# First tiles of the second matrix, tail weights and a fifth weight buffer in a macaron FFN–mixer encoder layer on one core

## Chip, core and metric

The kernel runs on one NeuronCore of a Trainium2 chip. The metric is the device time of one execution in microseconds (us). Three runs of the kernel before gave 1299.45 to 1301.09 us, with a median of 1300.53 us. A profile was taken of one more execution, which took 1301.27 us.

The core has engines that run side by side: TensorE (PE: matrix products, with weight loads as a row of their own, PEld), VectorE (DVE), ScalarE (ACT), GpSimd (POOL) and SyncE (SP), whose queue issues most of the transfers. Each engine takes its instructions in a fixed order. PE writes its results to eight PSUM banks.

## What is computed

One encoder layer over 512 positions with 16 meta tokens ahead of them (528 columns), 1024 channels, in float32. The second FFN needs only the 512 real columns.

```python
def swiglu(x, wi, wo):
    a, b = jnp.split(x @ wi, 2, axis=-1)
    return (jax.nn.silu(a) * b) @ wo
...
    h = jnp.concatenate([meta, x], axis=1)
    for l in range(DEPTH):
        n = norm_gains[l]
        h = h + 0.5 * rmsnorm(swiglu(rmsnorm(h, n[0]), ffn1_wi[l], ffn1_wo[l]), n[1])
        h = h + rmsnorm(hybrid_mixer(rmsnorm(h, n[2]), ...), n[3])
        h = h + 0.5 * rmsnorm(swiglu(rmsnorm(h, n[4]), ffn2_wi[l], ffn2_wo[l]), n[5])
    return h[:, N_META:]
```

The mixer has an input projection, three branches (a Fourier branch, a short convolution, and a delta rule that runs over chunks of 64 positions in both directions), and an output projection. The hidden width of each FFN is 2816, which is 22 tiles of 128 for `a` and 22 for `b`.

## The kernel before

Data lies with channels on the 128 partitions and positions along the free dimension, so 1024 channels are eight tiles (`KD`). A float32 factor is split into a rounded part and its rest: ACT casts (`wh`, `gh`, `x`'s first part), DVE subtracts (`wl`, `gl`, `x`'s second part). Each product is then three matmuls, written in `mm`. Every matmul of that kind carries line L144.

**Weights.** `load` fetches one weight tile into a staging tile `ws` (two of them), casts it on ACT and takes the rest on DVE (L230 and L231). The results `wh` and `wl` come from the pool `wp`, with four buffers each. `load` asks the scheduler to place this work earlier than written. `double` loads the weights for two output tiles of the second matrix at once.

**Order.** PE's instructions run as they are written. On the other engines a scheduler sets the order by priorities: `high_priority(n)` moves what is inside it n instructions up. `URGENT` is 450, `XAHEAD` 150.

**Stages.** `start` makes the first normalised input, and three units of the first matrix (a unit is one output tile over eight steps). `ffn` copies those raw (`raw`), makes five more units, and forms from them four gated tiles g = silu(a)·b (`silu`, `pair`; the split is at L235 and L236). `seven` scales the input (L555) and forms the sums that a Strassen-like scheme needs: it turns the two halves of the columns and of the channels into seven products. `rest` makes the last four splits of these sums. `both` computes two output tiles of the second matrix over the first four hidden tiles: all steps but the last of the two tiles, then the last step and the eviction of each. After the first `both` comes `rest`, then the second `both`. Then the long loop of Strassen products begins (`one`, `five`, `two`, `six`, `seven`, `four`), with second-matrix tiles between them. In FFN1 a tile has two halves of 264 columns, each in its own PSUM bank. In FFN2 both halves lie in one bank and matmuls are 512 wide, apart from the products and edges, which run 256 wide.

**Tail and edge.** The last hidden chunk goes through `tail`, whose eight output tiles are computed first for the first half of the columns, then for the second. `leave_y` copies a finished tile and adds its square to `acc`. `stat` turns `acc` into the factor of a norm: matmuls with ones, a square root on ACT, a reciprocal on DVE (L290), matmuls that spread the factor over the partitions, and a copy to `r` (L286). `edge` then makes the next stage's input: `step(i, k)` is, for half i and channel tile k, two DVE operations (L405, L407), an ACT copy (L411) and a DVE rest (L412). Three units of the next stage run on these inputs as they come: first half, then second. `early` puts the first half's `stat` between the matmuls of the second half's tail tiles. Edge 1 lies ahead of the mixer, edge 2 ahead of FFN2. `xstat` gathers the sums of squares of the new input (L302 on ACT, L303 on DVE) for the norm's factor `rx`. `finish` is the last norm.

The first term of `early`, the number of steps before the first half's `stat`, and the calls that set what runs first in an FFN are:

```python
            for _ in range(5):
                yield
            next(post[0])
...
        both(0, 0)
        with self.tc.high_priority(XAHEAD):
            rest()
        for m in range(2, FIRST, 2):
            both(0, m)
```

PSUM has two pools of four banks, `pb` (`big`) and `pd` (`dnp`). The mixer uses both, and shares `wp` with the FFNs.

## Time and profile before

| | |
|---|---|
| median of three runs | 1300.53 us (1299.45 to 1301.09) |
| profiled execution | 1301.27 us |
| its span in the trace | 1299.4 us |
| instructions in the trace | 22964 |
| mean granted TensorE clock | 0.996 |
| HBM read, written | 120.68 MB, 7.37 MB |

The profiled execution is 1.87 us longer than its span. Stages by the trace, in us from the span's start: start and first units to about 60; second-matrix first tiles to 74; loop of FFN1 to 357; its tail and edge 1 to 401; mixer to 880; output projection and edge 2 to 951; start of FFN2 to 994; its loop to 1262; finish to the end. A busy share by itself tells little here, since PE is busy nearly all of the time; the short stretches in which PE waits, or in which its clock is halved, are what can be read.

A line of a timeline is: start in us, duration in us, engine, line, operation, output and input, size, count, and in brackets the idle time ahead of it with what released it. A line of the windows view is: the stretch, its length, the busy time and number of instructions of PE, PEld, DVE, ACT and POOL, then the granted clock as a share of full speed, the DMA share and GB/s. A line of the waits view is: who waits for whom, us in total, number of waits, the longest.

### The profile page before, as it was taken

Reading aid. Unit: us, or ns where it says so; the run is one execution under the profiler, and the core shown is the slowest. Engines: PE = TensorE matmul, PEld = TensorE weight load, DVE = VectorE, ACT = ScalarE, POOL = GpSimd, SP = SyncE. Lnnn points to the kernel's source line nnn. Section 1 sums busy time; section 2 is a strip of 40 time slices with the busy share of each in tenths; the row PEclk is TensorE's granted clock in tenths of the full one; section 3 lists DMA queues with packets and bytes.
Section 4 is the critical chain, followed back from the end, with each engine's and each line's share of the span. In section 5 each row is a group of like instructions: output and inputs, shape, how many; then the busy total and the mean of one; then the engine's idle time right before and its main releaser. Section 6 shows DMA issues by size and latency. Waiting matters only on the chain.

```text
span 1299.4 us, 22964 instructions
## 1 busy us (share of the span) xinstructions
PE 1275.8 (98%) x9071; PEld 1157.2 (89%) x9071; DVE 942.5 (73%) x1867; ACT 615.9 (47%) x1208; POOL 13.4 (1%) x28
## 2 busy tenths in 40 slices
PE   9999999999999999999999999999999999999997
PEld 9999999999989988778977777887887999999997
DVE  7968777776568779658788678554789787777654
ACT  7555444434376543343632534334557554444436
POOL 0000000000000000000000000000100000000000
PEclk9999999999999999999999999999999999999999
DMA  7233333332244222312222212235433333333213
GB/s 250 80 106 99 98 98 98 98 101 71 82 163 160 82 82 73 110 63 82 66 66 66 66 58 73 82 97 178 147 117 102 107 106 99 106 98 94 86 49 130
DMA packets 70207, 129.53 MB, mean 100 GB/s; under 512 B 15820, under 2 KB 24140, under 8 KB 70100
## 3 DMA queue, kind: packets, MB, share of 16 engines
q1 hardware_dynamic: 64244, 124.40, 29.9%
q10 hardware_dynamic: 5088, 1.57, 0.5%
q0 software_dynamic: 768, 2.10, 0.4%
q8 instruction: 71, 1.16, 0.4%
q14 instruction: 36, 0.29, 0.1%
HBM read 120.68 MB, written 7.37 MB: 99 GB/s over the span
## 4 chain that ended last, share of the span: by engine, by line
PE 88%; DVE 7%; ACT 3%; issue 1%; DMA 1%; SPq 0%; DVEq 0%; ACTq 0%
PE pb L144 54%; PE pd L144 32%; DVE wl L231 1%; PE pd L148 1%; DVE acc L303 1%; DVE s L405 1%; ACT pb L346 1%; DVE h L407 1%; DVE x L412 0%; DMA ws<-in_wout 0%; ACT wh L230 0%; DVE l L236 0%; ACT sy L335 0%; DVE acc L336 0%; DMA h<-in_xT 0%
## 5 line engine op out<-in xcount | busy, mean ns | idle before, releaser
L144 PE MATMUL pb<-x,wh 128*128 128x264 f32 (+3 forms) x1568 | 357.4, 331 | 8.1 <-DVE x L412 3.6
L144 PEld LDWEIGHTS pb<-x,wh 128*128 128x128 f32 x1568 | 247.8, 190 | 40.9 <-DVE x L412 6.1
L144 PE MATMUL pb<-x,wl 128*128 128x264 f32 (+3 forms) x784 | 220.1, 326 | 0.0
L230 ACT CAST wh<-ws 128x1024 fp32r<-128x1024 f32 (+2 forms) x116 | 109.3, 945 | 176.5 <-PE pb L144 138.5
L144 PE MATMUL pd<-x,wh 128*128 128x264 f32 (+2 forms) x1040 | 192.1, 285 | 0.0
L235 ACT CAST wh<-wf 128x1024 fp32r<-128x1024 f32 x108 | 113.5, 1051 | 153.6 <-PE pd L144 122.3
L144 PE MATMUL pb<-gh,h 128*128 128x264 f32 (+1 forms) x768 | 172.8, 321 | 0.0
L144 PEld LDWEIGHTS pd<-x,wh 128*128 128x128 f32 x1040 | 160.5, 189 | 1.9
L236 DVE TENSOR_TENSOR wl<-wf,wh 128x1024 fp32r<-128x1024 f32 x108 | 132.0, 1223 | 39.4 <-ACT wh L235 39.0
L231 DVE TENSOR_TENSOR wl<-ws,wh 128x1024 fp32r<-128x1024 f32 (+2 forms) x116 | 126.2, 1090 | 33.1 <-ACT wh L230 32.7
L144 PEld LDWEIGHTS pb<-x,wl 128*128 128x128 f32 x784 | 134.1, 190 | 12.8 <-DVE wl L375 0.2
L144 PE MATMUL pd<-x,wl 128*128 128x264 f32 (+2 forms) x520 | 143.9, 284 | 0.0
L144 PEld LDWEIGHTS pb<-gh,h 128*128 128x128 f32 x768 | 120.9, 188 | 10.4
L144 PE MATMUL pb<-gl,h 128*128 128x264 f32 (+1 forms) x384 | 102.6, 321 | 0.0
L144 PEld LDWEIGHTS pd<-x,wl 128*128 128x128 f32 x520 | 96.3, 188 | 0.3
L144 PE MATMUL pd<-h,wh 128*128 128x264 f32 (+1 forms) x294 | 82.1, 282 | 0.0
L144 PE MATMUL pd<-l,wh 128*128 128x264 f32 (+1 forms) x288 | 81.5, 283 | 0.0
L144 PE MATMUL pd<-h,wl 128*128 128x264 f32 (+1 forms) x288 | 81.3, 282 | 0.0
L680 DVE TENSOR_TENSOR y<-y,pb 128x264 f32<-128x264 f32 (+1 forms) x128 | 48.7, 421 | 26.9 <-PE pb L144 26.9
L144 PEld LDWEIGHTS pb<-gl,h 128*128 128x128 f32 x384 | 63.6, 188 | 4.6
L144 PE MATMUL pb<-y,wh 128*128 128x512 f32 x192 | 61.7, 403 | 0.0
L230 ACT CAST h<-ws 128x1024 fp32r<-128x1024 f32 (+1 forms) x34 | 33.9, 1001 | 56.4 <-PE pb L144 50.5
(311 smaller groups left out, 2355.1 us busy)
## 6 DMA issues: line engine op xcount, KB each, us to landing
wf<-in_wi SPq DMA_DIRECT2D x144, 256.0 KB, 2.8
ws<-in_wo SPq DMA_DIRECT2D x64, 256.0 KB, 2.9
ws<-in_win SPq DMA_DIRECT2D x32, 512.0 KB, 3.2
ws<-in_wg SPq DMA_DIRECT2D x24, 512.0 KB, 3.2
ws<-in_wi SPq DMA_DIRECT2D x13, 512.0 KB, 3.3
ws<-in_wo SPq DMA_DIRECT2D x32, 192.0 KB, 2.5
ws<-in_wout SPq DMA_DIRECT2D x8, 512.0 KB, 3.2
h<-in_xT SPq DMA_DIRECT2D x10, 264.0 KB, 3.0
```

Source lines behind the costliest of these rows:

```text
L144: return self.e.matmul(out, lhsT, rhs, **kw)
L148: return self.e.transpose(*a)
L230: nc.scalar.copy(h[:, :n], st[:, :n])
L231: nc.vector.tensor_tensor(l[:, :n], st[:, :n], h[:, :n].bitcast(F32), op=ALU.subtract)
L235: self.nc.scalar.copy(h, src)
L236: self.nc.vector.tensor_tensor(l, src, h.bitcast(F32), op=ALU.subtract)
L303: V.tensor_tensor(acc, acc, sq, op=ALU.add)
L346: self.nc.scalar.copy(p, first[:, m, :w])
L405: V.scalar_tensor_tensor(t, ya[0][i][:, k, :W], self.gains[:, gpost, k:k + 1], r[:, c], op0=ALU.mult, op1=ALU.mult)
L407: V.tensor_tensor(hT[:, k, c], hT[:, k, c], t, op=ALU.add)
L680: V.tensor_tensor(y, y, p, op=ALU.add)
```

## The change

There are nine parts.

1. `wp` has five buffers of each of `wh` and `wl` instead of four.
2. `leave_y` takes the square of a tile before it copies the tile.
3. In `edge` after an FFN, the loads of the next stage's weights are written ahead of the tail tiles.
4. The first half's `stat` comes after seven steps of the second half's tail instead of five, in edge 1 and in `finish`.
5. `edge` serves as many units as it is given weights. Edge 2 is given four, so the unit of `wi[KF + 1]` leaves `ffn` and runs in the edge (48 matmuls of 256 columns instead of 24 of 512).
6. `xstat` in edge 2 has a priority of 60 instead of 450.
7. In `ffn`, scaling, silu and gating of the first three hidden tiles are urgent.
8. The four first tiles of the second matrix run together: all steps but the last of the four tiles, then the last step and eviction of each. The first two use `pd` banks. `rest` comes before them.
9. The tail's weights are split into the room of `h3` and `l3` (input sums of the Strassen scheme), no longer into `wp`.

```diff
-        self.wp = e(tc.tile_pool(name="wp", bufs=4))
+        self.wp = e(tc.tile_pool(name="wp", bufs=5))
...
-            if gain is None:
-                ACT.copy(y[i][:, m, :w], p)
-            else:
-                ACT.activation(y[i][:, m, :w], p, AF.Copy, scale=self.gains[:, gain, m:m + 1])
             if m == 0:
                 ACT.activation(acc[i], p, AF.Square)
             else:
...
+            if gain is None:
+                ACT.copy(y[i][:, m, :w], p)
+            else:
+                ACT.activation(y[i][:, m, :w], p, AF.Copy, scale=self.gains[:, gain, m:m + 1])
...
         tiles, tx, tc, more = tail()
+        if more:
+            ws = [self.load(a) for a in nxt]
         for t in tiles:
...
-            for _ in range(5):
+            for _ in range(7 if more else 5):
                 yield
...
-        ws = [self.load(a) for a in nxt]
-        os = [self.outs(C), self.outs(C), self.outs(C, self.dnp)]
+        if not more:
+            ws = [self.load(a) for a in nxt]
+        n = len(nxt)
+        os = [self.outs(C, self.dnp if i == 2 else None) for i in range(n)]
...
-            for j in range(3):
-                k = i - (LAG if j == 2 else 0)
+            for j in range(n):
+                k = i - (LAG if j >= 2 else 0)
...
-        self.xstat(C, hT, rx, *((XF, URGENT) if keep is not None else ()))
+        self.xstat(C, hT, rx, *((XF, 60) if keep is not None else ()))
...
-        for t, o in zip((a, b, a1), os):
+        for t, o in zip((a, b, a1, b1), os):
             self.raw(t, o)
-        o, o2, o3 = (self.unit(wi[i], x, C, new=n) for i, n in ((KF + 1, None), (2, None), (KF + 2, self.dnp)))
+        o = None if len(os) == 4 else self.unit(wi[KF + 1], x, C)
+        o2, o3 = self.unit(wi[2], x, C), self.unit(wi[KF + 2], x, C, new=self.dnp)
         self.drain()
-        for t in (a, b):
-            V.tensor_tensor(t[:, u], t[:, u], self.rx[:, u], op=ALU.mult)
-        silu(a)
-        pair(0, a[:, u], b[:, u])
...
+        with urgent():
+            for t in (a, b):
+                V.tensor_tensor(t[:, u], t[:, u], self.rx[:, u], op=ALU.mult)
+            silu(a)
+            pair(0, a[:, u], b[:, u])
...
-        both(0, 0)
-        with self.tc.high_priority(XAHEAD):
-            rest()
-        for m in range(2, FIRST, 2):
-            both(0, m)
+        ws = [double(0, m) for m in range(0, FIRST, 2)]
+        with self.tc.high_priority(XAHEAD):
+            rest()
+        us = [second(0, m, ws[m // 2], self.dnp if m < 2 else None) for m in range(FIRST)]
+        for ks, _, n in us:
             ks(range(n - 1))
-            ks2(range(n - 1))
+        for ks, evict, n in us:
             ks([n - 1])
             evict()
-            ks2([n - 1])
-            evict2()
...
-            ws = [double(fin, m) for m in range(0, KD, 2)]
+            q = KD * P * 3 // 4
+            h, l = (self.t(self.gp, i, [P, 3, 4, HN], F32R).rearrange("p a k c -> p (a k c)") for i in ("h3", "l3"))
+            at = lambda a, i: a[:, i * q:(i + 1) * q].rearrange("p (k c) -> p k c", c=P)
+            ws = [double(fin, m, (at(h, m // 2), at(l, m // 2))) for m in range(0, KD, 2)]
...
-        pre = k.edge(REAL, hT, ya, 3, 4, tail, to_ffn, [wi[0], wi[KF], wi[1]], k.keep)
+        pre = k.edge(REAL, hT, ya, 3, 4, tail, to_ffn, [wi[0], wi[KF], wi[1], wi[KF + 1]], k.keep)
```

Lines of the kernel after are shifted: L528 of before (the scaling of a unit out of its PSUM bank) is L532 after, L555 is L559, L627 (a times b) is L631, L640 and L643 are L646 and L649, L336 (the sum of squares) is L332, and the weight sums L603 to L609 are L607 to L613.

The change moves instructions on DVE at three places. The first is the start of FFN1 on DVE, before. `pb_389` and `pb_390` are the two banks of the unit `wi[KF + 1]`, `ev` are the tiles in which a and b are kept, and `h` is the input that `seven` scales.

```order
L528 TENSOR_TENSOR ev_376<-pb_389,rx_90 128x264
L555 SCALAR_TENSOR_TENSOR h_87<-h_87,gains_77,rx_90 128x528 x6
L231 TENSOR_TENSOR wl_743<-ws_741,wh_742 128x1024
L555 SCALAR_TENSOR_TENSOR h_87<-h_87,gains_77,rx_90 128x528 x2
L236 TENSOR_TENSOR l_78_725<-h_87,h_77_724 128x1056
L640 TENSOR_TENSOR ev_375<-ev_375,rx_90 128x528
L236 TENSOR_TENSOR l_78_725<-h_87,h_77_724 128x1056
L640 TENSOR_TENSOR ev_375<-ev_375,rx_90 128x528
L643 TENSOR_TENSOR ev_376<-ev_376,rx_90 128x528
L528 TENSOR_TENSOR ev_376<-pb_390,rx_90 128x264
```

The same place on DVE after the change:

```order
L532 TENSOR_TENSOR ev_376<-pb_389,rx_90 128x264
L231 TENSOR_TENSOR wl_743<-ws_741,wh_742 128x1024
L646 TENSOR_TENSOR ev_375<-ev_375,rx_90 128x528 x2
L649 TENSOR_TENSOR ev_376<-ev_376,rx_90 128x528
L532 TENSOR_TENSOR ev_376<-pb_390,rx_90 128x264
L559 SCALAR_TENSOR_TENSOR h_87<-h_87,gains_77,rx_90 128x528
```

The eight scalings of the input and two of its splits, which stood between the two banks, now come behind the second bank, one or three at a time among the gating of the first tiles.

The second place is edge 1 on DVE, before: the first steps of the first half, from the reciprocal of its norm on. `wl` with 1024 elements are the splits of the mixer's first three weight tiles, `acc_740` the second half's sum of squares.

```order
L290 RECIPROCAL rt_4382<-rt_4382 88x3
L336 TENSOR_TENSOR acc_740<-acc_740,sy_4389 128x264
L231 TENSOR_TENSOR wl_4544<-ws_4542,wh_4543 128x1024
L336 TENSOR_TENSOR acc_740<-acc_740,sy_4404 128x264
L405 SCALAR_TENSOR_TENSOR s_4414<-y_737,gains_77,r_4206 128x264
L405 SCALAR_TENSOR_TENSOR s_4419<-y_737,gains_77,r_4206 128x264
L336 TENSOR_TENSOR acc_740<-acc_740,sy_4439 128x264
L407 TENSOR_TENSOR h_4197<-h_4197,s_4414 128x264
L407 TENSOR_TENSOR h_4197<-h_4197,s_4419 128x264
L231 TENSOR_TENSOR wl_4550<-ws_4548,wh_4549 128x1024
L336 TENSOR_TENSOR acc_740<-acc_740,sy_4454 128x264
L412 SCALAR_TENSOR_TENSOR x_4208<-h_4197,gains_77,x_4207 128x264
```

And on DVE after:

```order
L290 RECIPROCAL rt_4406<-rt_4406 88x3
L332 TENSOR_TENSOR acc_740<-acc_740,sy_4415 128x264
L405 SCALAR_TENSOR_TENSOR s_4432<-y_737,gains_77,r_4206 128x264
L405 SCALAR_TENSOR_TENSOR s_4437<-y_737,gains_77,r_4206 128x264
L407 TENSOR_TENSOR h_4197<-h_4197,s_4432 128x264
L407 TENSOR_TENSOR h_4197<-h_4197,s_4437 128x264
L332 TENSOR_TENSOR acc_740<-acc_740,sy_4450 128x264
L405 SCALAR_TENSOR_TENSOR s_4442<-y_737,gains_77,r_4206 128x264
L412 SCALAR_TENSOR_TENSOR x_4208<-h_4197,gains_77,x_4207 128x264
```

The three weight splits now stand ahead of the first sum of squares; from the reciprocal to the first half's sixth rest none is left.

The third place is the end of edge 2 on DVE, before: the last three rests of the second half and what stands around them. `sx` are the squares that `xstat` adds, and `wf` the weight tiles of FFN2's first pair, of which L603 and its kind form sums.

```order
L405 SCALAR_TENSOR_TENSOR s_10342<-y_9677,gains_77,r_9873 128x256
L303 TENSOR_TENSOR acc_10380<-acc_10380,sx_10394 128x256
L412 SCALAR_TENSOR_TENSOR x_9875<-h_9674,gains_77,x_9874 128x256
L303 TENSOR_TENSOR acc_10380<-acc_10380,sx_10397 128x256
L412 SCALAR_TENSOR_TENSOR x_9875<-h_9674,gains_77,x_9874 128x256
L407 TENSOR_TENSOR h_9674<-h_9674,s_10342 128x256
L603 TENSOR_TENSOR wf_10728<-wf_10728,wf_10731 128x512
L303 TENSOR_TENSOR acc_10380<-acc_10380,sx_10400 128x256
L412 SCALAR_TENSOR_TENSOR x_9875<-h_9674,gains_77,x_9874 128x256
```

The same place on DVE after the change, up to the last rest but one:

```order
L609 TENSOR_TENSOR wf_10748<-wf_10747,wf_10749 128x512
L303 TENSOR_TENSOR acc_10406<-acc_10406,sx_10426 128x256
L303 TENSOR_TENSOR acc_10429<-acc_10429,sx_10431 128x256
L405 SCALAR_TENSOR_TENSOR s_10370<-y_9671,gains_77,r_9867 128x256
L303 TENSOR_TENSOR acc_10429<-acc_10429,sx_10434 128x256
L611 TENSOR_TENSOR wf_10749<-wf_10750,wf_10749 128x512
L303 TENSOR_TENSOR acc_10429<-acc_10429,sx_10437 128x256
L407 TENSOR_TENSOR h_9668<-h_9668,s_10370 128x256
L303 TENSOR_TENSOR acc_10429<-acc_10429,sx_10440 128x256
L613 TENSOR_TENSOR wf_10750<-wf_10748 128x512
L303 TENSOR_TENSOR acc_10429<-acc_10429,sx_10443 128x256
L412 SCALAR_TENSOR_TENSOR x_9869<-h_9668,gains_77,x_9868 128x256
```

Before, the sums of squares stood one or two at a time between the rests from the first half on. Now all fourteen stand behind the second half's third rest, and the four weight sums among them.

More of the change, by code (lines that the diff above doesn't have):

```diff
@@ L446, in edge @@
             step(1, k)
-            for j in range(3):
+            for j in range(n):
                 self.mm(os[j].half[1:], ws[j], x, k, k, k == 0, k == KD - 1)
-        self.xstat(C, hT, rx, *((XF, URGENT) if keep is not None else ()))
+        self.xstat(C, hT, rx, *((XF, 60) if keep is not None else ()))
         return x, os
@@ L473, in early @@
         def early():
-            for _ in range(5):
+            for _ in range(7):
                 yield
@@ L634, in ffn @@
         a, b, a1, b1 = e0[:, 0], e0[:, 1], e1[:, 0], e1[:, 1]
-        for t, o in zip((a, b, a1), os):
+        for t, o in zip((a, b, a1, b1), os):
             self.raw(t, o)
-        o, o2, o3 = (self.unit(wi[i], x, C, new=n) for i, n in ((KF + 1, None), (2, None), (KF + 2, self.dnp)))
+        o = None if len(os) == 4 else self.unit(wi[KF + 1], x, C)
+        o2, o3 = self.unit(wi[2], x, C), self.unit(wi[KF + 2], x, C, new=self.dnp)
         self.drain()
-        for t in (a, b):
-            V.tensor_tensor(t[:, u], t[:, u], self.rx[:, u], op=ALU.mult)
-        silu(a)
-        pair(0, a[:, u], b[:, u])
-        V.tensor_tensor(a1[:, u], a1[:, u], self.rx[:, u], op=ALU.mult)
-        silu(a1)
-        self.scaled(b1, o)
-        pair(1, a1[:, u], b1[:, u])
-        e = self.ev()
-        self.scaled(e[:, 0], o2)
-        silu(e[:, 0])
-        self.scaled(e[:, 1], o3)
-        pair(2, e[:, 0, u], e[:, 1, u])
+        with urgent():
[3 more added lines that the diff above has]
+            pair(0, a[:, u], b[:, u])
+            V.tensor_tensor(a1[:, u], a1[:, u], self.rx[:, u], op=ALU.mult)
+            silu(a1)
+            if o is None:
+                V.tensor_tensor(b1[:, u], b1[:, u], self.rx[:, u], op=ALU.mult)
+            else:
+                self.scaled(b1, o)
+            pair(1, a1[:, u], b1[:, u])
+            e = self.ev()
+            self.scaled(e[:, 0], o2)
+            silu(e[:, 0])
+            self.scaled(e[:, 1], o3)
+            pair(2, e[:, 0, u], e[:, 1, u])
         e = self.ev()
@@ L663, in ffn, with second @@
         later = []
-        def second(ci, m, w):
+        def second(ci, m, w, new=None):
             n = len(CHUNKS[ci])
-            o = self.outs(C)
+            o = self.outs(C, new)
             def ks(r):
@@ L687, in double @@
             return self.load([wo[i][:, c.start:c.stop] for i in (m, m + 1)], len(c), to)
-        def both(ci, m):
-            w = double(ci, m)
-            (ks, evict, n), (ks2, evict2, _) = second(ci, m, w), second(ci, m + 1, w)
+        ws = [double(0, m) for m in range(0, FIRST, 2)]
[3 more added lines that the diff above has]
+        for ks, _, n in us:
             ks(range(n - 1))
-            ks2(range(n - 1))
+        for ks, evict, n in us:
             ks([n - 1])
             evict()
-            ks2([n - 1])
-            evict2()
-        both(0, 0)
-        with self.tc.high_priority(XAHEAD):
-            rest()
-        for m in range(2, FIRST, 2):
-            both(0, m)
         hx = self.t(self.xp, "h", [P, KD, L], F32R).rearrange("p k c -> p (k c)")
```

## The prediction

> **What bounds the kernel now.** I read the page's engine shares first, then its chain of work that ended last, then PE's waits, and last the windows, cut at the places where PE waits.
>
> ```profile
> PE 1275.8 (98%) x9071; PEld 1157.2 (89%) x9071; DVE 942.5 (73%) x1867; ACT 615.9 (47%) x1208; POOL 13.4 (1%) x28
> ...
> PE 88%; DVE 7%; ACT 3%; issue 1%; DMA 1%; SPq 0%; DVEq 0%; ACTq 0%
> ```
>
> PE is busy for 98% and is 88% of the chain that ended last, so the matmuls themselves set the time. The change takes none of them away. What it can win is in the other 12% of the chain, where PE waits for DVE or ACT.
>
> ```profile
> PE pb L144 <- DVE x L412: 3.6, 9, 0.8
> PE pb L144 <- DVE ev L528: 2.8, 1, 2.8
> PE pb L144 <- DVE gl L236: 1.7, 2, 1.2
> ...
> PE pd L144 <- DVE acc L336: 0.8, 1, 0.8
> PE pb L144 <- ACT x L411: 0.8, 1, 0.8
> PE pd L144 <- DVE rt L290: 0.7, 1, 0.7
> ```
>
> These rows sum to 10.4 us, and each belongs to an FFN's start, an edge or the finish. The windows add what such waits do to the clock:
>
> ```profile
> 40.00:47.00 7.00, 4.69 (x39) 4.47 (x37) 7.00 (x10) 4.17 (x5) 0.00 (x0) 1.00 0.25 75
> 47.00:51.00 4.00, 3.56 (x18) 3.56 (x19) 3.92 (x7) 2.19 (x4) 0.00 (x0) 0.57 0.30 78
> 51.00:74.00 23.00, 21.78 (x177) 21.39 (x175) 21.21 (x27) 14.20 (x21) 0.00 (x0) 1.00 0.15 49
> ...
> 366.00:381.00 15.00, 12.42 (x97) 11.30 (x95) 10.74 (x24) 14.42 (x37) 0.20 (x2) 1.00 0.36 106
> 381.00:388.00 7.00, 6.51 (x42) 6.31 (x43) 5.25 (x14) 2.87 (x8) 0.00 (x0) 0.76 0.51 203
> ...
> 412.00:880.00 468.00, 466.05 (x3094) 386.66 (x3093) 348.20 (x912) 195.38 (x430) 4.26 (x6) 1.00 0.25 78
> ...
> 910.00:953.00 43.00, 40.08 (x305) 37.20 (x304) 34.48 (x82) 25.20 (x62) 8.77 (x16) 1.00 0.39 129
> 953.00:1000.00 47.00, 45.51 (x217) 37.26 (x217) 41.98 (x50) 28.89 (x43) 0.00 (x0) 1.00 0.32 101
> ```
>
> In 40–47 and 51–74 DVE is busy nearly throughout while PE is not: there DVE is the bound. In 468 us of the mixer PE idles 1.95 us. Twice PE's clock drops, to 0.57 over 4 us and to 0.76 over 7 us, which costs 4.0·0.43 = 1.7 us each time (7.0·0.24 = 1.7).
>
> **Term 1, start of FFN1: −4.9 us.** The rows of PE, then of DVE:
>
> ```profile
> 44.41 0.28 PE L144 MATMUL pb<-x,wh 128*128 128x264 f32 x1
> 47.44 1.03 PE L144 MATMUL pb<-x,wh 128*128 128x264 f32 x3 [2.75 <-DVE ev L528]
> ...
> 66.78 0.51 PE L144 MATMUL pb<-gl,wh 128*128 128x264 f32 x2 [1.22 <-DVE gl L236]
> ...
> 74.00 0.65 PE L144 MATMUL pd<-h,wh 128*128 128x264 f32 x4
> ```
> ```profile
> 35.52 0.43 DVE L528 TENSOR_TENSOR ev<-pb,rx 128x264 f32<-128x264 f32 x1
> 36.19 4.17 DVE L555 SCALAR_TENSOR_TENSOR h<-h,gains,rx 128x528 f32<-128x528 f32 x6 [0.24 <-ACT rx L286]
> ...
> 46.96 0.43 DVE L528 TENSOR_TENSOR ev<-pb,rx 128x264 f32<-128x264 f32 x1
> ...
> 67.81 1.22 DVE L236 TENSOR_TENSOR wl<-wf,wh 128x1024 fp32r<-128x1024 f32 x1
> ```
>
> PE waits 2.75 us for a bank that DVE empties at 46.96, because the eight scalings of h and two splits of them stand ahead. Urgent gating moves these behind it: now one weight split and three scalings of `ev` stand there, about 1.2 + 3·0.6 = 3 us from 36, so the bank is free near 39.5 and PE needs it at 44.5. The wait goes, with the half clock behind it (1.6). The wait for `gl` goes too, since 72 matmuls of 0.12 us (the four at 74.00 take 0.65, 0.28 of it the last one's length), four tiles by three steps, now run ahead of the fourth `gl`, where 36 did. PE would then reach the first loop product (74.00) about 6.2 us sooner, at 67.8.
>
> DVE's work has only been re-ordered, though. From 36.2 on, 42 operations up to and with the first product's weight split stand in the new order, 31.3 us by their sizes: 0.34 us for 264 columns from start to start, 0.6 to 0.7 for 528, 1.15 for 1024 and more (the 27 of the window 51–74 take 21.21, 0.79 each, which would be 33). With an estimated 1.6 us for what DVE still waits for on PE and ACT it ends at 69.1, where before it started at 67.81. So a new wait of 1.3 us takes part of the gain: −6.2 + 1.3 = **−4.9**, between −3.5 (DVE 1.4 us later still) and −6.2 (no new wait).
>
> **Term 2, edge 1: −3.5 us.**
>
> ```profile
> 371.30 1.22 DVE L231 TENSOR_TENSOR wl<-ws,wh 128x1024 fp32r<-128x1024 f32 x1 [0.50 <-ACT wh L230]
> ...
> 377.32 1.22 DVE L231 TENSOR_TENSOR wl<-ws,wh 128x1024 fp32r<-128x1024 f32 x1
> ```
> ```profile
> 368.53 0.63 PE L144 MATMUL pd<-ones,acc 128*88 128x1 f32 x6 [0.81 <-DVE acc L336]
> ...
> 379.34 0.39 PE L144 MATMUL pb<-x,wh 128*128 128x264 f32 x1 [0.70 <-DVE x L412]
> ...
> 380.99 0.39 PE L144 MATMUL pb<-x,wh 128*128 128x264 f32 x1 [0.78 <-ACT x L411]
> 381.87 0.59 PE L144 MATMUL pb<-x,wh 128*128 128x264 f32 x1 [0.49 <-DVE x L412]
> ```
>
> Three weight splits (the rows above are the first and the last) lie between the factor r and the inputs x that PE waits for: 3·1.22 us on DVE, 3.4 by start-to-start times. Issued earlier, they lie under the tail, where DVE has idle time. Squares ahead of copies and `stat` two steps later take the 0.81 us, and give r a head start of about 1 us. The stretch 366–388 holds 2.58 + 0.49 us of idle PE and the 1.7 us of half clock, 4.8 in all. Two other weight splits now enter the second half's chain, and later steps are paced by DVE, so I take **−3.5**, between −1.5 and −5. The tail's weights in the sums' room I cost at nothing: the products that read this room come ahead of the last second-matrix tiles in PE's order, and these tiles hide the casts; without that cover the first tail tile would wait for one cast and split, some 2 us. One load more ahead on SP delays reloads of h that nobody waits for yet.
>
> **Term 3, edge 2 and start of FFN2: −4.8 us.**
>
> ```profile
> 950.98 0.63 PE L144 MATMUL pb<-x,wh 128*128 128x512 f32 x2
> 951.45 0.40 PE L144 MATMUL pb<-x,wl 128*128 128x512 f32 x1
> ...
> 983.14 0.50 PE L144 MATMUL pb<-gh,wh 128*128 128x512 f32 x1 [0.98 <-ACT gh L235]
> 984.14 0.51 PE L144 MATMUL pb<-gl,wh 128*128 128x512 f32 x1 [0.50 <-DVE gl L236]
> ...
> 993.80 0.64 PE L144 MATMUL pd<-h,wh 128*128 128x256 f32 x4
> ```
> ```profile
> 948.35 0.68 DVE L603 TENSOR_TENSOR wf<-wf,wf 128x512 f32<-128x512 f32 x1
> 948.98 0.43 DVE L303 TENSOR_TENSOR acc<-acc,sx 128x256 f32<-128x256 f32 x1
> 949.38 0.48 DVE L412 SCALAR_TENSOR_TENSOR x<-h,gains,x 128x256 fp32r<-128x256 f32 x1
> ```
>
> Before, three units end at 950.98 and the fourth at 956.6: its 24 matmuls start 0.233 us apart (two from 950.98 to 951.45), 5.6 us. In the edge it is the same work, 48 matmuls of 256 columns, 0.118 us apart (four in 0.64 us at 993.80, 0.28 of it the last one's length), 5.7 us. But four units give PE 12 matmuls a step (1.42 us), while a step costs DVE three operations (0.40 + 0.34 + 0.40 = 1.14 by start-to-start times, as the 0.40 from 949.38 to what follows there) without the add of squares, and 1.47 with it. Behind the rest in DVE's queue stands the next step's work, and PE's units wait for it. So PE, no longer DVE, paces the edge, until the moved adds come: fourteen of 0.34 and four weight sums of 0.6 (948.35 to 948.98) stand among the last rests, 7.2 us that no cover hides in full. I estimate new waits of 1.7 and 1.1 us there, and the end at 953.9: −2.7. The waits for gating (983.14, 984.14) go, with their refill 2.1 us, since gating no longer stands behind eight scalings of h (4.17 us for six, in the row at 36.19) and two splits. DVE's chain to the first product (last unit's scaling, silu, product, cast, split, then six operations of 1.15) ends about where PE arrives, at 989.0. Sum **−4.8**: −3 if the late adds stall more, −6 if they stall nothing.
>
> **Term 4, finish: −0.4 us.**
>
> The wait for `rt` (0.7 in the list of waits) stays, since `stat` still comes four steps ahead of its use; leftover transposes now run behind the last matmuls and under ACT's last square, some 0.4 us: between −0.9 and +0.1.
>
> **The fifth buffer: 0.** PE's order in the mixer is unchanged and its idle time there is 1.95 us, so no more than that can come. It can cost, see the third rival. I keep −1.5 to +2.
>
> The sum is −4.9 − 3.5 − 4.8 − 0.4 = −13.6 us. Against the profiled execution (span 1299.4 and 1.87 around it, 1301.27) this gives 1287.7; that execution lay 0.74 above the median of the runs, so I say **1287.0**.
>
> **Rivals.** *DVE takes the place of the wait.* In both FFN starts DVE was nearly full (21.21 of 23, 41.98 of 47 us). If its chain to the first product is 1.4 us longer at FFN1 and 3.8 at FFN2, and edge 1 stays paced by DVE, terms 1 to 3 are −3.5, −1.0 and −1.5: with the finish −6.4, so 1294. Against it: the trace's idle time of PE is longer than the new chain in each case.
>
> *The clock falls anew.* The waits of edge 1 that end at 381.87 (0.70, 0.78 and 0.49 within some 3 us) were enough for 3.4 us at half clock (7.0·0.24/0.5). The new waits at the end of edge 2 (1.7 and 1.1) are as long. If they set one off, and edge 1's stays (1.3 of its term), the time is +1.7 + 1.3: 1290.
>
> [...]
>
> *Slower: the fifth buffer lets weight splits in ahead of the delta rule.*
>
> ```profile
> L231 DVE TENSOR_TENSOR wl<-ws,wh 128x512 fp32r<-128x512 f32 (+1 forms) x76 | 79.8, 1050 | 6.3 <-ACT wh L230 5.8
> ...
> L1427 DVE SCALAR_TENSOR_TENSOR vp<-pd,neg_eg,vn 64x128 f32<-64x128 f32 x60 | 20.8, 349 | 6.4 <-PE pd L144 4.9
> ```
>
> In the mixer (this is its DVE by lines) 76 splits share in-order DVE with the 60 updates of the delta rule, four heads to a step: 15 steps. A load that starts one buffer earlier can put 1.05 us of split, and its cast on ACT, ahead of an update that PE waits for. From 16.2/15 = 1.08 us a step on, the change is slower by over 0.2%; at 1.2 it gives +18, 1305. Against it: PE finds other work during these steps, as its 1.95 us of idle time say.
>
> *The change does not do what it says.* If the waits only move to the next operand on DVE at both FFN starts, edge 1's smaller bound and the finish are left, −1.9: 1298.6.
>
> **How the numbers follow.** Chances: forecast 0.55, DVE 0.18, clock 0.12, no effect 0.08, slower 0.07. The first three are faster by over 0.2% (2.6 us, about what a measurement of this kernel can tell from no change): 0.85, same 0.08, slower 0.07. The terms' own bounds give −19.6 (1281) and, with +2 in the mixer, −5.9 (1294.6). The range 1281 to 1296 takes in these and the two milder rivals.
>
> **What would show it.** Right: the first Strassen product of FFN1 near 69, with a short wait for a weight split or none; no wait of PE for the scaling out of a bank, nor for `gl`; one stretch of half clock less; edge 1 ends some 8 us sooner, 5 of them from the start; waits for x only at the end of edge 2; the first product of FFN2 some 13 us sooner. Mixer as long as before. Wrong: a mixer longer by more than 2 us, a first product later than 71, or waits for x all through edge 2.

## The result and the profile after

The kernel after takes 1290.63 us (median of four runs, 1290.36 to 1291.84). The kernel before took 1300.81 us beside it (four runs, 1299.45 to 1303.67). The ratio is 0.9921 with a 95% interval of 0.9903 to 0.9939. The profiled execution took 1290.73 us with a span of 1288.6 us.

PE's chain and its waits, from the page and the waits view of the kernel after (a row of the waits: who waits for whom, us in total, times, the longest):

```profile
PE 1268.7 (98%) x9095; PEld 1154.6 (90%) x9095; DVE 944.0 (73%) x1867; ACT 616.8 (48%) x1209; POOL 13.4 (1%) x28
...
PE 86%; DVE 7%; ACT 3%; issue 2%; DMA 1%; SPq 0%; DVEq 0%; ACTq 0%
```
```profile
PE pb L144 <- DVE x L412: 2.3, 5, 0.7
PE pb L144 <- ACT h L230: 2.1, 1, 2.1
PE pb L144 <- ACT x L411: 1.1, 1, 1.1
...
PE pd L144 <- DVE acc L332: 1.0, 1, 1.0
...
PE pd L144 <- DVE rt L290: 0.6, 1, 0.6
...
PE pb L144 <- DVE h L231: 0.5, 1, 0.5
```

The waits for `ev` (2.8 us before), for `gl` (1.7) and for `gh` (1.0) are gone. A wait that was not there before is the second longest entry: PE waits 2.1 us for ACT's cast of `h` at L230, and 0.5 us for DVE's rest at L231. Here `h` is a weight tile of the second matrix that lies in the room of the old input.

Where the time went is read by laying the same matmul of both traces side by side. The numbers below are differences of start times (after minus before), and each stage's share is the change of that difference across it.

| stage | difference behind it, us | share, us | forecast, us |
|---|---|---|---|
| first units, to about 11 us | +0.57 | +0.6 | 0 |
| start of FFN1 to its loop | −5.42 | −6.0 | −4.9 |
| edge 1 | −7.58 | −2.2 | −3.5 |
| mixer, to the output projection | −10.47 | −2.9 | 0 |
| edge 2, start of FFN2, to its first product | −14.48 | −4.0 | −4.8 |
| first ten us of FFN2's loop | −9.92 | +4.6 | 0 |
| finish | −10.85 | −0.9 | −0.4 |

The first row is scatter: the same place varies by some 1.5 us among the traced runs of kernels that do not differ there. PE's wait for `wh` at L374, at its end, is 0.2 us in the kernel before, 0.8 in the kernel after and 1.4 in the variant with the tail's weights in the pool. The two first products of the loops, one in each FFN, carry the largest part. The timeline of PE after (start, duration, operation):

```profile
68.43 0.66 PE L144 MATMUL pd<-h,wh 128*128 128x264 f32 x4
68.93 0.28 PE L144 MATMUL pd<-l,wh 128*128 128x264 f32 x1
69.06 0.39 PE L144 MATMUL pd<-h,wl 128*128 128x264 f32 x1
...
979.31 0.63 PE L144 MATMUL pd<-h,wh 128*128 128x256 f32 x4
```

They stood at 74.00 and 993.80 before. And the windows after (the clock stands ahead of the last two numbers):

```profile
40.00:47.00 7.00, 7.00 (x59) 7.00 (x59) 6.85 (x14) 4.44 (x6) 0.00 (x0) 1.00 0.20 68
47.00:51.00 4.00, 4.00 (x35) 4.00 (x34) 4.00 (x6) 1.87 (x3) 0.00 (x0) 1.00 0.35 108
...
360.00:375.00 15.00, 13.99 (x115) 13.55 (x115) 9.74 (x26) 14.69 (x42) 0.20 (x2) 1.00 0.34 115
...
900.00:945.00 45.00, 42.14 (x344) 40.90 (x343) 35.01 (x83) 25.49 (x60) 8.77 (x16) 1.00 0.37 129
...
979.00:990.00 11.00, 11.00 (x74) 10.02 (x73) 11.00 (x12) 7.20 (x15) 0.00 (x0) 1.00 0.39 119
990.00:1000.00 10.00, 7.36 (x25) 5.31 (x24) 8.49 (x10) 6.24 (x10) 0.00 (x0) 0.83 0.57 170
```

Both stretches of half clock of before (0.57 near 47, 0.76 near 381) are gone. A new one stands at 990–1000, where the clock is 0.83, with 2.64 us of idle PE in the same ten microseconds. Ahead of it DVE is busy for 11.00 of 11 us. The chain of work through this place, in order of time (start, us, what):

```profile
984.14 2.27 DVE x L236 x2
986.41 1.13 DVE x L583
987.55 1.13 DVE h L575
988.68 0.60 DVE wf L609
989.28 0.58 DVE wf L611
...
990.95 0.81 DVE wl L236
...
992.08 1.16 DVE wl L236
993.24 1.20 DVE h L231
...
994.48 3.71 PE pb L144 x9
```

The chain runs on DVE until 994.4 and only then on PE. The `x` rows are the last splits of the input sums, written by `rest`. They still read the old input, whose room the weight tile is to take. The last of them and the cast into that room, from the timelines of DVE and ACT:

```profile
989.81 1.22 DVE L236 TENSOR_TENSOR x<-h,x 128x1024 fp32r<-128x1024 f32 x1
992.09 2.01 ACT L230 CAST h<-ws 128x1024 fp32r<-128x1024 f32 x2
```

The read ends at 991.03 and the cast starts at 992.09. In the 1.06 us between, ACT is busy throughout (1.06 us) with work that stands ahead of the cast: the casts of `wh` at L235 and a copy at L691.

### The profile page after: what moved, and what is told of

Read it like the earlier page. It is cut to its first block, busy times and chain, and to the rows that moved or that the text cites. A ratio compares the mean times of both kernels' runs of the same rounds, so it can differ in the third digit from the quotient of the medians.

```text
span 1288.6 us, 22995 instructions
## 1 busy us (share of the span) xinstructions
PE 1268.7 (98%) x9095; PEld 1154.6 (90%) x9095; DVE 944.0 (73%) x1867; ACT 616.8 (48%) x1209; POOL 13.4 (1%) x28
## 4 chain that ended last, share of the span: by engine, by line
PE 86%; DVE 7%; ACT 3%; issue 2%; DMA 1%; SPq 0%; DVEq 0%; ACTq 0%
PE pb L144 52%; PE pd L144 32%; DVE wl L231 1%; PE pd L148 1%; ACT wh L230 1%; DMA ws<-in_win 1%; DVE acc L303 1%; DVE wl L236 0%; DVE s L405 0%; DVE x L412 0%; DVE h L407 0%; ACT sy L331 0%; DMA h<-in_xT 0%; DVE h L559 0%; DMA ws<-in_wout 0%
## 5 line engine op out<-in xcount | busy, mean ns | idle before, releaser
L144 PE MATMUL pb<-gh,h 128*128 128x264 f32 (+2 forms) x864 | 202.2, 320 | 2.6 <-ACT h L230 2.1
L235 ACT CAST wh<-wf 128x1024 fp32r<-128x1024 f32 x108 | 113.5, 1052 | 147.1 <-PE pd L144 122.0
L230 ACT CAST wh<-ws 128x1024 fp32r<-128x1024 f32 (+1 forms) x108 | 102.7, 953 | 165.1 <-PE pb L144 138.1
L144 PEld LDWEIGHTS pb<-gh,h 128*128 128x128 f32 x864 | 139.7, 189 | 14.1 <-ACT h L230 2.5
L231 DVE TENSOR_TENSOR wl<-ws,wh 128x1024 fp32r<-128x1024 f32 (+1 forms) x108 | 118.6, 1100 | 36.1 <-ACT wh L230 36.0
L144 PE MATMUL pb<-gl,h 128*128 128x264 f32 (+2 forms) x480 | 130.1, 314 | 0.0
L144 PEld LDWEIGHTS pb<-gl,h 128*128 128x128 f32 x480 | 82.1, 189 | 4.7
L230 ACT CAST h<-ws 128x1024 fp32r<-128x1024 f32 (+1 forms) x42 | 40.6, 974 | 62.5 <-PE pb L144 51.5
```

The costliest lines, as they stand in the source:

```text
L144: return self.e.matmul(out, lhsT, rhs, **kw)
L230: nc.scalar.copy(h[:, :n], st[:, :n])
L231: nc.vector.tensor_tensor(l[:, :n], st[:, :n], h[:, :n].bitcast(F32), op=ALU.subtract)
L235: self.nc.scalar.copy(h, src)
```

## The experiments

Differences of stages below are read as in the table, between traces of the kernels named. A halved clock is counted at 1.7 us, an estimate from the windows: 4.0·0.43 at 47–51 before, 10.0·0.17 at 990–1000 after. It came in some traces and not in others where the waits were nearly the same (last section), so where one trace of a pair has it in the stage compared, the text says so.

### Second pair of weights out of the old input's room

```diff
-                ready[i] = double(*line[i], (room[i // 2 % 2], room[2 + i // 2 % 2]) if i else None)
+                ready[i] = double(*line[i], (room[i // 2 % 2], room[2 + i // 2 % 2]) if i > 2 else None)
```

> The changed kernel, but the second pair of second-matrix weights in each FFN loop goes into the weight pool instead of the room of the old input h. Theory A (the new wait of 2.1 + 0.55 us near 993 and the half clock behind it come from that room, which the last splits of the input sums still read): the wait goes, the first loop tiles of FFN2 run without a gap, and the time falls by some 4.5 us to about 1286. Theory B (DVE is simply full there, and the split of these weights comes late in whatever buffer): the wait stays within 1 us of its size, time about 1290.

Measured: 1285.88 us (1285.2 to 1287.54), 0.9884 of the kernel before (0.987 to 0.9899). The loop of FFN2 runs 4.6 us ahead of the changed kernel's from 998 on; before 990 the two differ by 0.3 us or less. PE's waits for `h` are gone from the list. The windows of this run:

```profile
979.00:990.00 11.00, 11.00 (x74) 10.03 (x73) 11.00 (x11) 7.88 (x15) 0.00 (x0) 1.00 0.52 167
990.00:1000.00 10.00, 10.00 (x59) 8.76 (x58) 9.73 (x11) 7.93 (x14) 0.00 (x0) 1.00 0.48 153
```

DVE is as full as it was (11.00 of 11 us in 979–990), yet PE no longer waits, and the clock stays at 1.00. So theory A holds and B falls: it is the room, not DVE's load alone. DVE's load matters through the room, since it decides when the last reader of the old input is done.

### Four weight buffers instead of five

```diff
-        self.wp = e(tc.tile_pool(name="wp", bufs=5))
+        self.wp = e(tc.tile_pool(name="wp", bufs=4))
```

> The changed kernel with four weight buffers instead of five. Theory A (the 2.9 us that the mixer became shorter come from the fifth buffer): the mixer is 2.9 us longer again, time about 1293.5. Theory B (they come from another part, or from the phase in which the mixer starts): mixer as in the changed kernel, time about 1290.6.

Measured: 1290.23 us (1289.14 to 1290.79). The mixer is 2.6 us longer than in the changed kernel (the difference goes from −1.37 at its start to +1.27 at the output projection), as theory A has it. The time is nevertheless the same. Up to FFN2's loop this kernel falls behind by as much as 4.3 us, and then it gains nearly all of that back, for it arrives late enough not to wait for `h` at L230, and waits 0.3 us for `h` at L231. The mixer is theory A's and the time theory B's; neither foresaw both.

### Five buffers in the kernel before, and nothing else

```diff
-        self.wp = e(tc.tile_pool(name="wp", bufs=4))
+        self.wp = e(tc.tile_pool(name="wp", bufs=5))
```

> The kernel before with five weight buffers and nothing else. Theory A (the fifth buffer lets weight splits of the mixer start one load earlier, and this shortens waits of PE there): the mixer is 2 to 3 us shorter, the other stages are as before within 1 us, time 1298 to 1299. Theory B (the rival of the prediction: early splits stand ahead of the delta rule's updates): the mixer is longer.

Measured: 1298.91 us (ten runs, 1296.4 to 1301.57), a ratio of 0.9987 (0.9976 to 0.9998). In the traced run, one of the fastest (1296.66), the mixer is 3.1 us shorter than before, as theory A says; and the start of FFN1 is 2.8 us shorter, which it does not say. Of these, 1.1 us come behind PE's wait for `ev`: the wait is as long as before (3.0 us against 2.8), but the clock stays at 1.00 (last section). The other 1.7 us come where the wait for `gl` (1.22 us before) is gone. PE's weight loads for the delta rule's updates show the buffers' part. From the waits of the kernel before, with four buffers:

```profile
PEld pd L144 <- DVE vp L1427: 4.1, 15, 0.4
PEld pd L144 <- ACT vp L1442: 2.5, 6, 0.7
```

From this run, with five:

```profile
PEld pd L144 <- ACT vp L1442: 3.0, 7, 0.7
PEld pd L144 <- DVE vp L1427: 2.5, 7, 0.4
```

The changed kernel has the same 3.0 and 2.5, and its variant with four buffers the same 4.1 and 2.5. These two rows show 1.1 us of the 2.6 to 3.1. Laid side by side, the mixer's gain stands at the same few places in the changed kernel and in this one. For the changed kernel it is 0.8 us at each of two steps of the delta rule (near 552 and 735 us), 0.9 between 774 and 794, and 0.7 where the output projection starts and PE's wait for `mh` falls from 1.06 to 0.37 us; two other steps lose 0.4. At the first of these places, on PE before and after the change:

```profile
559.79 1.28 PE L144 MATMUL pd<-vp,EZ 64*64 64x128 f32 x8
```
```profile
552.20 0.65 PE L144 MATMUL pd<-vp,EZ 64*64 64x128 f32 x8
```

The same eight matmuls take half as long, and neither row has idle time in it.

### Three units in edge 2

```diff
-        pre = k.edge(REAL, hT, ya, 3, 4, tail, to_ffn, [wi[0], wi[KF], wi[1], wi[KF + 1]], k.keep)
+        pre = k.edge(REAL, hT, ya, 3, 4, tail, to_ffn, [wi[0], wi[KF], wi[1]], k.keep)
```

> The changed kernel with three units in edge 2, the fourth made after it as before. Theory A (what PE gains in edge 2 it waits for later, since DVE bounds the start of FFN2 up to the weights in the room): edge 2 and the first product come 2.7 us later, the wait near 993 becomes shorter by about as much, time 1290 to 1291. Theory B (the two add up): time about 1293.3.

Measured: 1289.75 us (1288.6 to 1291.38), not slower than the changed kernel. The start of FFN2 is 3.3 us later, and the wait for `h` at L230 is gone. Some 1.7 us of the 3.3 are a halved clock in edge 2 (0.57 over 935–939, 4.0·0.43) that the changed kernel's trace does not have (1.00 over the same stretch). Theory A holds in the time and in the wait: what the fourth unit gains in the edge, PE waited for later. Its size is not shown apart from the clock.

### The sums of squares of edge 2 at the old priority

```diff
-        self.xstat(C, hT, rx, *((XF, 60) if keep is not None else ()))
+        self.xstat(C, hT, rx, *((XF, URGENT) if keep is not None else ()))
```

> The changed kernel with the sums of squares of edge 2 at the old priority. Both theories: the three waits at the end of edge 2 (0.88, 1.30, 0.40 us) go, short waits of 0.1 to 0.7 us at each step take their place. Theory A (spreading the adds is worth more than crowding them at the end): the edge ends 1 to 2.5 us sooner, but the time stays at 1290 to 1291, since the wait near 993 takes it back. Theory B (crowded adds are better, DVE paces every step otherwise): the edge ends 1 us later or more.

Measured: 1291.31 us (1289.94 to 1293.47). Edge 2 ends 0.3 us sooner against its own start, and the wait at L230 stays at 2.1 us. Neither theory's size is met. Spread or crowded, the adds cost the edge about the same.

### No urgency for the first hidden tiles

```diff
-        with urgent():
+        with self.tc.high_priority(0):
             for t in (a, b):
```

> The changed kernel without the urgency of the first three hidden tiles of each FFN. Theory A (this urgency is what empties the bank in time and brings the gated tiles early): PE's wait of 2.7 us near 44.5 is back with its half clock, the first product of FFN1 comes 4 us or more later, near 72.5 or after, and waits for gh or gl are back in FFN2. Theory B (four tiles at once give enough cover by themselves): first product of FFN1 within 1 us of 68.4.

Measured: 1307.53 us (1305.6 to 1308.83), a ratio of 1.0053 (1.0038 to 1.0068): slower than the kernel before. The waits of this run:

```profile
PE pd L144 <- ACT gh L235: 6.4, 3, 3.6
PE pb L144 <- DVE ev L532: 4.8, 1, 4.8
PE pd L144 <- DVE gl L236: 2.7, 3, 1.5
```

FFN1's loop starts 6.5 us later than in the changed kernel, counted from its own 11 us mark. FFN2's first product comes 14 us later, counted from the end of edge 2. Theory A holds. This one part carries the starts of both FFNs, and without it the other eight lose more than they win. In the windows, DVE is busy for 24.42 of 25 us while PE idles for 9.11 and its clock is 0.76:

```profile
965.00:990.00 25.00, 15.89 (x52) 10.68 (x52) 24.42 (x34) 13.81 (x17) 0.00 (x0) 0.76 0.23 74
```

### The four first tiles two by two

```diff
-        for ks, _, n in us:
-            ks(range(n - 1))
-        for ks, evict, n in us:
-            ks([n - 1])
-            evict()
+        for q in (us[:2], us[2:]):
+            for ks, _, n in q:
+                ks(range(n - 1))
+            for ks, evict, n in q:
+                ks([n - 1])
+                evict()
```

> The changed kernel with the four first tiles of the second matrix two by two, as before, all else kept (the early splits of the input sums, the other banks, the urgency). Theory A (the urgency already brings the fourth gl early; running four tiles together adds little): first product of FFN1 within 0.6 us of 68.4, and the same at FFN2. Theory B (it is the four tiles' 72 matmuls that cover the fourth gl, as the prediction put it): the wait of some 1.2 us is back in FFN1 and some 1 us in FFN2.

Measured: 1290.34 us (1289.56 to 1293.16). FFN1's first product comes 0.9 us later against the same start, and in FFN2 a wait of 0.6 us for `gl` is back. So the cover of four tiles is worth 0.9 us at FFN1, between the two theories. In FFN2 this kernel is 0.7 us behind the changed one's at 990 and 0.9 ahead of it at 1000. Its waits for the room are nearly the same there (1.72 and 0.70 us), but the clock is 1.00, where the changed kernel's is 0.83:

```profile
990.00:1000.00 10.00, 7.58 (x32) 5.53 (x31) 10.00 (x13) 6.03 (x10) 0.00 (x0) 1.00 0.50 156
```

So what comes back in FFN2 is mostly the clock, and the equal time does not show that the four tiles are worth nothing.

### The factor after five steps

```diff
-            for _ in range(7 if more else 5):
+            for _ in range(5):
...
-            for _ in range(7):
+            for _ in range(5):
```

> The changed kernel with the first half's norm factor after five steps again, in edge 1 and in the finish. Theory A (PE still waits there for the last sum, and what sets the edge is when the factor and the inputs come from DVE): PE waits 0.7 us longer at the sums' matmul, edge 1 ends within 0.3 us of the changed kernel's. Theory B (the two steps of cover are won in full): edge 1 ends 0.7 us later. The finish loses up to 0.5 us, by both.

Measured: 1292.38 us (1290.69 to 1293.44). Edge 1 ends 1.7 us later and the finish loses 0.9 us. PE's wait for the last sum is 1.76 us, 0.8 us longer than in the changed kernel. Right behind it the clock is halved in this run (0.72 over 364–370; in the changed kernel it is 1.00 over 360–375). That costs about 1.7 us (6.0·0.28), as much as the edge lost, so the trace does not show what the two steps are worth apart from the clock, and it does not decide between the theories.

### The tail's weights in the pool, and the mixer's loads late

Two kernels undo one part each of what the change does ahead of edge 1. The first:

```diff
-            h, l = (self.t(self.gp, i, [P, 3, 4, HN], F32R).rearrange("p a k c -> p (a k c)") for i in ("h3", "l3"))
...
-            ws = [double(fin, m, (at(h, m // 2), at(l, m // 2))) for m in range(0, KD, 2)]
+            ws = [double(fin, m) for m in range(0, KD, 2)]
```

> The changed kernel with the tail's split weights in the weight pool again, all else kept. Theory A (it is this part that lets the mixer's first weight splits leave the first steps of edge 1, since the pool's buffers are no longer taken by the tail): two splits of 1.1 us stand among the first rests of edge 1 again, the edge ends 1 to 2 us later, time 1291 to 1292.5. Theory B (as the prediction costed it, this part is worth nothing; the loads written ahead of the tail do it): edge 1 within 0.4 us of the changed kernel's.

The second writes the mixer's first loads behind the tail again:

```diff
-        if more:
-            ws = [self.load(a) for a in nxt]
         for t in tiles:
...
-        if not more:
-            ws = [self.load(a) for a in nxt]
+        ws = [self.load(a) for a in nxt]
```

> The changed kernel with the loads of the mixer's first weights written behind the tail again, all else kept. Theory A (the tail's room does it, the place of these loads in the program does nothing): edge 1 within 0.4 us of the changed kernel's, time 1290.6. Theory B (the prediction's term 2: the loads written ahead of the tail take the splits out of the chain): edge 1 ends 1 to 3 us later.

Measured: 1293.56 us (1291.14 to 1295.46) for the first, 1290.56 us (1289.95 to 1290.8) for the second. With the tail's weights in the pool edge 1 ends 1.7 us later; with the loads late it loses 0.02 us (this run lay 0.34 us behind the changed kernel's ahead of the edge, and 0.36 behind it; that lag arose in the first matmuls of the tail). Theory A holds in both as to the edge. The first kernel's time is above theory A's 1292.5, and 1.3 us of it are a halved clock in edge 2 (0.57 over 944–948; last section). DVE's timeline with the tail's weights in the pool:

```profile
364.21 0.17 DVE L290 RECIPROCAL rt<-rt 88x3 f32<-88x3 f32 x1
365.14 1.23 DVE L231 TENSOR_TENSOR wl<-ws,wh 128x1024 fp32r<-128x1024 f32 x1 [0.76 <-ACT wh L230]
369.23 1.22 DVE L231 TENSOR_TENSOR wl<-ws,wh 128x1024 fp32r<-128x1024 f32 x1
370.71 0.49 DVE L412 SCALAR_TENSOR_TENSOR x<-h,gains,x 128x264 fp32r<-128x264 f32 x1
```

And in the changed kernel, with no weight split between the reciprocal and the first rest:

```profile
365.18 0.17 DVE L290 RECIPROCAL rt<-rt 88x3 f32<-88x3 f32 x1
369.82 0.48 DVE L412 SCALAR_TENSOR_TENSOR x<-h,gains,x 128x264 fp32r<-128x264 f32 x1
```

The reciprocal comes 1.0 us later in the changed kernel, and the first rest 0.9 us sooner: the two splits, 1.14 us each from start to start, are about the 1.9 between them.

### Ten steps, and a longer gap in the finish

On top of the first experiment:

```diff
-            for _ in range(7 if more else 5):
+            for _ in range(10 if more else 5):
...
             next(st)
-            for _ in range(4):
+            for _ in range(6):
```

> The kernel of the first experiment (second pair of weights in the pool), and in edge 1 the first half's factor after ten steps instead of seven; in the finish six steps instead of four between the sums and their use. Theory A (PE waits there for a sum whose time is set by ACT and DVE; three more steps of matmuls cover it and delay nothing): PE's wait of 1.0 us for the last sum and most of that of 0.6 us for the reciprocal in the finish go; edge 1 ends about 1 us sooner, time about 1284.3. Theory B (the factor itself comes later by the three steps): edge 1 unchanged or later, time 1285.5 to 1286.5.

Measured: 1286.41 us (1285.82 to 1287.34), no better than the first experiment's 1285.88. The finish gains 1.1 us, as A has it. Edge 1 loses 2.4 us against its own start. PE's timeline of this run:

```profile
364.79 0.39 PE L144 MATMUL pb<-gh,h 128*128 128x264 f32 x1 [1.50 <-ACT pb L346]
365.25 0.62 PE L144 MATMUL pd<-ones,acc 128*88 128x1 f32 x6
...
368.52 1.04 PE L144 MATMUL pd<-ident,rt 88*128 88x88 f32 x6
```

The wait for the last sum is gone, but PE reaches the next tail tile sooner, waits 1.50 us there for ACT to bring the tile's sum so far into PSUM, and has the factor's matmuls (`rt`) 2.3 us later than the first experiment. ACT is the bound there (14.69 of 15 us busy in the changed kernel's window 360–375). Behind that wait the clock is halved in this run (0.58 over 365–369, where the changed kernel has 1.00), which is about 1.7 us (4.0·0.42). The mean clock of the whole trace is 0.997 here and 0.998 in the first experiment. If that one kept full clock at this place, the 1.7 are part of the 2.4 us. Neither theory had this wait; B's time is met.

### The sums of squares behind the rests

On top of the kernel just shown:

```diff
-        self.xstat(C, hT, rx, *((XF, 60) if keep is not None else ()))
+        self.xstat(C, hT, rx, *((XF, 0) if keep is not None else ()))
```

> The kernel of the third run of this group, with the sums of squares of edge 2 at priority 0, so that they stand behind the rests. Theory A (DVE, which is busy without a gap from 960 to 990, bounds the start of FFN2): edge 2 ends up to 1.9 us sooner with its waits gone, but the first product of FFN2 or the first loop tiles wait for as much, and the time is within 0.7 us of that run's. Theory B (PE bounds the start once the room is free): the first product comes 1.5 to 2 us sooner, time about 1282.5.

Measured: 1284.22 us (1283.79 to 1284.79), 0.9866 of the kernel before (0.985 to 0.9883), and the fastest kernel of the study. Edge 2 and the start of FFN2 gain 2.6 us. The window of edge 2 in this run:

```profile
900.00:945.00 45.00, 44.12 (x363) 43.26 (x361) 33.54 (x78) 24.91 (x57) 8.80 (x16) 1.00 0.39 132
```

PE idles 0.88 us in it, where the changed kernel idles 2.86, and no wait follows at the first product. Theory B holds: with the room free, PE bounds the start. Its time of 1282.5 is missed, since it took the ten steps for a gain. Edge 1 loses 2.3 us against the changed kernel's in this run too, about 1.7 of it with a halved clock (0.57 over 367–371, where the changed kernel has 1.00). A version with seven steps was not tried.

## Why the prediction held, and where its sum was off

The time lies in the range, and the direction and most of the places were right. The sum forecast −13.6 us; the measured difference is −10.2. That it came so near owes something to luck: in the traces the mixer and the start of FFN1 gave 4.0 us more than forecast, and the first microseconds of FFN2's loop, edge 1 and edge 2 6.7 us less. The time is nearer to the 1290 of the second rival than to 1287.0, and the clock did fall anew (0.83 over 990–1000), but behind another wait than that rival named.

**Start of FFN1 (forecast −4.9, measured −6.0).** Both waits and the half clock went, as said (1.00 over 47–51, 0.57 before). The weight split that the forecast put at 69.1 ended at 69.0 (started 67.79, 1.22 long), so the working of DVE's new order was exact. The step that failed is the price set on it, 1.3 us. The first product begins with matmuls that need the split's other half only, and its first use of `wl`, at 69.06, found it just done.

**Edge 1 (forecast −3.5, measured −2.2).** The three splits left the first steps, as said. The step that named their cause was wrong: it credited the loads written ahead of the tail and costed the tail's room at nothing. Undoing the loads costs nothing, undoing the room 1.7 us. A second step failed too: PE's wait for the last sum, 0.81 us before, was to go with squares ahead of copies and two steps more. It is 1.01 us. What the two steps are worth is not shown (the trace with five has a halved clock, 0.72 over 364–370), and the order of square and copy was not tested alone. Of what the edge gained, up to 1.7 us may be the halved clock of before (0.76 over 381–388).

**Mixer (forecast 0, measured −2.9).** This term was mis-sized, and outside its bounds. The step that failed took PE's idle time in the mixer, 1.95 us of 468, for the most that could be won. The fifth buffer won 2.6 to 3.1 us there, in both kernels. Of the 2.9 us, 0.7 lie at the wait for `mh`, just behind the window in which the forecast counted. The other 2.2 came while the idle time counted stayed what it was, 1.95 us before and 1.94 after. The gain did not show as idle time of PE: the eight matmuls above took 1.28 us before and 0.65 after, with no idle time in either row, and PEld's waits show 1.1 us of it. The third rival, early splits that delay the delta rule, did not come about: with five buffers these waits are shorter in sum (5.5 us instead of 6.6).

**Edge 2 and start of FFN2 (forecast −4.8, measured −4.0).** Edge 2 gave −2.0 (forecast −2.7) and the gating behind it −2.0 (forecast −2.1). Waits stand at the end of edge 2, as said, 0.7 and 1.1 us (forecast 1.7 and 1.1). The gating's waits are gone.

**First microseconds of FFN2's loop (forecast nothing, measured +4.6).** This is what the sum lacked. The first rival had the mechanism, DVE in place of the wait that goes, but it looked for it at the first product. PE passes the first product without a wait and stops 14 us behind it, at a weight tile whose room is free only when the last of DVE's splits has read the old input. The forecast asked what is late next at the first product and not behind it. With that tile elsewhere the time is 1285.88 us, 1.1 below what was forecast. About 1.6 of the 4.6 us are the halved clock behind the wait, since the kernel with two by two tiles has nearly the same waits (1.72 and 0.70 us) at a clock of 1.00 and loses 3.0.

**Finish (forecast −0.4, measured −0.9).** The wait for `rt` stays, 0.6 us. With five steps the finish loses 0.9 us, so the two steps are its gain.

**Clock.** The second rival did not occur in the changed kernel's trace: the new waits at the end of edge 2 (0.72 and 1.14 us) left the clock at 1.00, and edge 1's half clock went (1.00 over 380–404). That was partly luck. With the tail's weights in the pool nearly the same two waits (0.73 and 1.18 us) came with a halved clock, 0.57 over 944–948. A new stretch at half clock came with the wait at 993 instead (0.83 over 990–1000), and is gone in the first experiment, where that wait is gone (1.00).

## What to carry to other kernels

When an engine is moved forward by several microseconds, follow it past the first operand it used to wait for, up to every buffer that is free only after the last reader on the engine that did not move. A wait that goes can come back many microseconds later at such a buffer (here 14 us behind the first product), and an experiment that gives that one tile another place shows it at once. A stage's idle time was no upper bound for what could be won in it (the mixer gave 2.9 us with 1.95 us of idle PE): read the starts of the same matmuls in both traces. And set the granted clock beside every difference of 1 or 2 us between two traces; here a halved clock cost an estimated 1.7. Parts of a change that each look like a gain may depend on one of them: here eight parts without the urgency were slower than none.

## What the runs showed of the hardware

In the cases below the clock fell behind waits of 0.5 to 2.8 us. The wait of 2.10 us at 993.20, followed by one of 0.55, came with a granted clock of 0.83 over 990–1000, an estimated 3.4 us at half (10.0·0.17/0.5); waits of 0.72 and 1.14 us within 3 us at the end of edge 2 left it at 1.00 over 934–945:

```profile
939.44 0.39 PE L144 MATMUL pb<-x,wh 128*128 128x256 f32 x1 [0.72 <-DVE x L412]
942.14 0.91 PE L144 MATMUL pb<-x,wh 128*128 128x256 f32 x2 [1.14 <-ACT x L411]
...
993.20 0.51 PE L144 MATMUL pb<-gh,h 128*128 128x512 f32 x1 [2.10 <-ACT h L230]
...
994.48 1.22 PE L144 MATMUL pb<-gh,h 128*128 128x512 f32 x2 [0.55 <-DVE h L231]
```

Before, three waits of 0.5 to 0.8 us within some 3 us at edge 1 had come with the same loss (0.76 over 381–388, 7.0·0.24 = 1.7 us).

The length of a wait alone does not tell these cases apart. With the tail's weights in the pool the waits at the end of edge 2 are 0.73 and 1.18 us, and the clock is 0.57 over 944–948. The wait for `ev` is 2.75 us in the kernel before, and the clock is 0.57 over 47–51 behind it; with five buffers and nothing else it is 3.03 us, and the clock stays at 1.00. The kernel before, then the one with five buffers:

```profile
43.68:47.09 3.41, 1.01 (x9) 0.79 (x7) 3.41 (x6) 2.94 (x4) 0.00 (x0) 1.00 0.18 68
47.09:50.50 3.41, 3.06 (x14) 3.06 (x15) 3.33 (x6) 2.10 (x4) 0.00 (x0) 0.50 0.25 64
```
```profile
42.68:46.09 3.41, 1.86 (x16) 1.65 (x14) 3.41 (x5) 2.90 (x3) 0.00 (x0) 1.00 0.00 0
46.09:49.51 3.42, 1.94 (x16) 1.94 (x17) 3.42 (x6) 3.01 (x5) 0.00 (x0) 1.00 0.02 5
```

Over its two rows PE idles for 2.75 us in the kernel before and for 3.03 us with five buffers; the clock falls, to 0.50, in the first case alone. No run here varies such a wait alone, so what decides whether the clock falls is not shown.

In these runs a kernel's times also spread with its mean clock: the kernel before with five buffers took 1296.4 to 1296.95 us in its four runs with a clock of 0.998, and 1298.29 to 1301.57 us in the others.
